# Four-layer fp32 block on one core: gates by tokens, output product by halves, convolutions by taps, head evacuations behind the norm

## The chip, the cores and the metric

The kernel runs on one core of a Trainium2 chip, as one launch. The metric is the device time of that launch in microseconds (us). Each core has a matrix engine, TensorE (PE), whose weight loads are listed apart (PEld), and VectorE (DVE), ScalarE (ACT), GpSimd (POOL) and SyncE (SP), which here issues all loads. PE writes its results to PSUM (the tiles called bank); everything else lies in SBUF.

## The reference, cut to what matters

The input is 256 tokens of width 1024 in fp32. It passes through two layers of one kind (here a0, a1) and two of another (b0, b1). Of each layer the part that the change touches is the mixer: a projection of the normed input feeds four branches, and the branches are merged by gates:

```python
# layers a: four branches of width 512
ys = jnp.stack([y_ssm, y_fox, y_moba, y_dsa], axis=2)
proj = jnp.einsum('bsnc,ncd->bsnd', ys, w_branch)
gates = jax.nn.sigmoid(h @ w_gate + b_gate).reshape(bsz, seq, N_BRANCH, D_MODEL)
merged = jnp.sum(gates * proj, axis=2)
return merged @ w_out

# layers b: four branches of width 256, gates without a bias
proj = jnp.einsum('bsnw,nwd->bsnd', branches, w_branch)
gate = jax.nn.sigmoid(gates).reshape(b, s, N_BRANCH, D_MODEL)
merged = jnp.sum(gate * proj, axis=2)
return merged @ w_out
```

In layers b one branch (deltanet) first runs a causal depthwise convolution of four taps and a silu over 768 channels, `silu(causal_depthwise_conv(concat(q, k, v), conv_w))`, and another (spatial gating) a gelu and `u * (mixed + b_s)`. After the mixer, layers a have a swiglu network, layers b a cross-attention over 256 memory tokens and a squared-relu network. Each sub-block begins with an rmsnorm.

## The kernel before, in words

**Products.** PE's fast fp32r form is not exact enough alone, so each fp32 product is made of three matmuls (`mm3`): low half of the left operand by high half of the right, high by low, high by high, all into one PSUM bank. Weights come from memory in chunks of two row tiles of 128 by 512 columns (512 KB) into one of a few `raw` buffers; ACT rounds a chunk to its high half (`high`, `rt<-raw`), DVE subtracts to get the low half (`low`, `rt<-raw,rt`), and PE uses the pair. Pairs are prepared `LOOK = 5` ahead, in the order of `plan`. Two loops use them. `g1` holds a tile of 128 tokens still and streams 512 weight columns: the result has tokens on partitions. `g2` holds 128 weight columns still and streams the 256 tokens: the result has channels on partitions.

**Order.** All instructions are emitted by one program that runs twice: a dry run gives the time at which each chunk is due, the second run emits. Between the matmuls of a product, `tick` prepares chunks (`advance`) and lets other work step forward: generators in named queues, "lanes" (`spawn`, `lane`), which yield where they would wait. `Model` holds a clock of each engine, and a lane steps when the model says that its inputs are there. A lane spawned with a key is stepped before `advance` does its part, and `flush(key)` runs it to its end. `scoped` runs something at once. `drain` runs lanes dry. Each engine executes its instructions in the order in which they were emitted.

**Stages of a layer.** `head` runs the first products of a mixer: for each of the two token halves it flushes the norm's lane of that half (`h0`, `h1`), runs `g1` on each named block and evacuates it at once. In layers a the blocks are misc (320 columns that get a rope, 16 and 4 more) and mq (512 columns, with a rope); `rope` is two multiplications on DVE from PSUM and an addition on POOL. Then come further blocks with the branches as lanes between them. `mix` runs over the four branches in a set order and two column halves c: `gate` (`g2`, 96 matmuls of 256 columns, then tanh on ACT, in layers a with a bias per channel, which is a bias per partition), `proj` (`g2` on the branch's output, DVE multiplies with the gate, POOL or DVE adds to the sum), and after the last branch `fin` splits the sum, which is in the form that the next product needs, into high and low halves. `out_a` and `out_b` run the output product by `g1` and `g11`, per column half c over all 8 row tiles, and flush `mT0` to `mT3` (the pieces of the sum) as they come to them.

**Convolutions and spatial gate in layers b.** `convs` runs `g2` for two groups of 128 channels and spawns `conv`: ACT writes the last tap, `acc = src * w3`, and DVE adds the three others, one operation per tap and group, each reading PSUM:

```python
for i in range(2):
    for j in (1, 2, 3):
        self.stt(av[:, i, j:], src[:, i, :256 - j], wts[i][:, 3 - j:4 - j], av[:, i, j:], OP.mult, OP.add)
self.fbank(bank)
```

There are three such convolutions a layer. `sgu` evacuates the spatial gate with four operations of 64 columns, one per group; `gelu` has two passes before its tanh.

**Lines and names.** All engine operations are recorded on line L362 (a helper), loads on L434. Tile names: `raw` a weight chunk, `rt` a high or low half, `ft` anything else in SBUF, `bank` PSUM, `qt` small matrices in another form, `junk` results that nobody reads. A row of 128x1024 with `rt<-raw,rt` on DVE is the low half of a whole chunk; 128x512 is half a chunk. The third layer of the kernel is b0.

## Time and profile before

| what | value |
|---|---|
| runs, median of 3 | 2286.72 us (2281.83 to 2288.86) |
| the profiled execution, its own time | 2281.47 us |
| its span on the core | 2279.7 us |
| mean granted PE clock | 0.993 |
| matmuls | 16244 |
| instructions | 40153 |
| read from memory | 371.81 MB |

The span is the time from the first to the last instruction that the hardware profiler recorded; the execution's own time has some 1.8 us around it. Busy times are given per engine, with the share of the span. A waiting engine is put down to the one whose semaphore came last. The granted clock is the share of full speed that PE was given: its two levels are 1.2 and 2.4 GHz, so a stretch at 0.65 holds both.

### The profile page before, as it was taken

The numbers are of one execution on the slowest core, as the hardware profiler recorded it, in microseconds if no ns is written. First come the engines' busy times: TensorE is split into PE (matmuls) and PEld (weight loads), VectorE is DVE, ScalarE is ACT, GpSimd is POOL, SyncE is SP. The second block draws the span as 40 slices with busy tenths as digits, with TensorE's granted clock in tenths as the row PEclk, the third lists the DMA queues.
The fourth block names the chain that finished last, engine by engine and source line by source line (L and its number), as shares of the span: only waits on it lengthen the run. The fifth ranks groups of instructions, "written<-read, shape, count | busy, mean of one in ns | idle before, by whom it ended". The sixth has DMA issues, their size and how long they took to land. (4 is left out here: it accounts for less than half of the span.)

```text
span 2279.7 us, 40153 instructions
## 1 busy us (share of the span) xinstructions
PE 2232.7 (98%) x16244; PEld 2015.1 (88%) x16244; DVE 1526.0 (67%) x2509; ACT 1073.2 (47%) x1695; POOL 267.0 (12%) x244
## 2 busy tenths in 40 slices
PE   8999999999899999999998999999999899999998
PEld 6888998999788899899888899988988889998897
DVE  7887567546798756665678767455567877745554
ACT  4555545434455554444454335454445433544543
POOL 2102110000301111000112220000001222000000
PEclk9999999999999999999999999999999999999999
DMA  6444565655444456565534256446653424644563
GB/s 228 149 130 148 163 196 183 206 193 164 147 130 139 148 172 203 197 211 179 167 112 149 77 162 207 157 151 234 205 157 106 153 80 157 207 162 151 194 206 109
DMA packets 106662, 375.47 MB, mean 165 GB/s; under 512 B 12474, under 2 KB 12908, under 8 KB 106476
## 3 DMA queue, kind: packets, MB, share of 16 engines
q1 hardware_dynamic: 106476, 372.91, 49.9%
q8 instruction: 127, 2.08, 0.4%
q14 instruction: 59, 0.48, 0.1%
HBM read 371.81 MB, written 1.05 MB: 164 GB/s over the span
## 5 line engine op out<-in xcount | busy, mean ns | idle before, releaser
L362 PE MATMUL bank<-rt 128*128 128x256 f32 (+2 forms) x12720 | 1996.2, 316 | 20.5 <-DVE rt L362 20.4
L362 PEld LDWEIGHTS bank<-rt 128*128 128x128 f32 x12720 | 1778.5, 192 | 176.1 <-DVE rt L362 26.7
L362 DVE TENSOR_TENSOR rt<-raw,rt 128x1024 fp32r<-128x1024 f32 (+2 forms) x692 | 834.0, 1229 | 347.2 <-ACT rt L362 345.8
L362 ACT ACTIVATE rt<-raw 128x1024 fp32r<-128x1024 f32 (+2 forms) x692 | 694.7, 1033 | 366.7 <-PE bank L362 211.8
L362 POOL TENSOR_TENSOR ft<-ft 128x512 f32<-128x512 f32 (+6 forms) x186 | 213.0, 1154 | 1847.4 <-DVE ft L362 1578.0
L362 PE MATMUL bank<-ft 64*64 64x64 f32 (+13 forms) x3476 | 312.9, 264 | 19.6 <-DVE ft L362 13.5
L362 PEld LDWEIGHTS bank<-ft 64*64 64x64 f32 (+6 forms) x3476 | 240.3, 146 | 78.1 <-DVE ft L362 19.6
L362 ACT ACTIVATE ft<-bank 128x512 f32<-128x512 f32 (+4 forms) x256 | 135.2, 536 | 305.2 <-PE bank L362 292.5
L362 ACT ACTIVATE ft<-ft 128x128 f32<-128x128 f32 (+7 forms) x206 | 87.5, 435 | 189.5 <-DVE ft L362 181.3
L362 DVE SCALAR_TENSOR_TENSOR ft<-ft 128x512 f32<-128x512 f32 (+5 forms) x211 | 93.1, 462 | 37.0 <-ACT junk L362 20.2
L362 DVE TENSOR_TENSOR ft<-ft 128x512 f32<-128x512 f32 (+5 forms) x122 | 69.9, 575 | 63.3 <-ACT ft L362 58.3
L362 ACT ACTIVATE rt<-bank 128x512 fp32r<-128x512 f32 (+1 forms) x98 | 53.5, 553 | 99.8 <-PE bank L362 99.4
L362 DVE SCALAR_TENSOR_TENSOR ft<-bank,ft 128x255 f32<-128x255 f32 (+6 forms) x176 | 80.2, 482 | 26.5 <-PE bank L362 10.0
L362 DVE TENSOR_TENSOR ft<-ft,bank 64x512 f32<-64x512 f32 (+3 forms) x92 | 59.4, 645 | 40.3 <-PE bank L362 37.0
L362 ACT ACTIVATE ft<-bank,ft 128x256 f32<-128x256 f32 x108 | 47.1, 480 | 78.8 <-PE bank L362 49.1
L362 DVE SCALAR_TENSOR_TENSOR ft<-ft,bank 128x512 f32<-128x512 f32 (+1 forms) x106 | 67.5, 641 | 19.7 <-PE bank L362 9.7
L362 ACT ACTIVATE rt<-ft 128x512 fp32r<-128x512 f32 x62 | 39.1, 630 | 81.1 <-DVE ft L362 76.6
L362 DVE COPY ft<-bank 128x384 f32<-128x384 f32 (+5 forms) x96 | 49.3, 541 | 31.4 <-PE bank L362 28.7
L362 DVE TENSOR_SCALAR ft<-ft 128x256 f32<-128x256 f32 (+7 forms) x236 | 56.7, 284 | 19.9 <-ACT ft L362 8.9
L362 DVE TENSOR_TENSOR ft<-bank,ft 128x512 f32<-128x512 f32 (+8 forms) x124 | 50.4, 442 | 18.4 <-PE bank L362 9.7
L362 DVE SCALAR_TENSOR_TENSOR rt<-bank,rt 128x512 fp32r<-128x512 f32 (+1 forms) x72 | 43.3, 612 | 17.2 <-ACT rt L362 17.0
L362 ACT ACTIVATE junk<-ft 128x512 bf16<-128x512 f32 (+1 forms) x46 | 27.2, 591 | 57.4 <-DVE ft L362 53.2
(37 smaller groups left out, 314.8 us busy)
## 6 DMA issues: line engine op xcount, KB each, us to landing
raw<-in_wts_a SPq DMA_DIRECT2D x340, 512.0 KB, 4.3
raw<-in_wts_b SPq DMA_DIRECT2D x312, 512.0 KB, 4.2
raw<-in_wts_b SPq DMA_DIRECT2D x24, 256.0 KB, 2.7
raw<-in_wts_b SPq DMA_DIRECT2D x8, 440.0 KB, 4.0
raw<-in_wts_a SPq DMA_DIRECT2D x8, 340.0 KB, 4.4
ft<-in_mem SPq DMA_DIRECT2D x4, 512.0 KB, 7.8
ft<-in_x SPq DMA_DIRECT2D x2, 512.0 KB, 3.4
ft<-in_norm_mix_pre SPq DMA_DIRECT2D x2, 512.0 KB, 5.3
```

The source lines that it names most:

```text
L362: r = None if self.dry else f(*args, **kw)
```

## The change

It has six parts.

1. **Gates and projections by tokens.** `mix` uses `g1` in place of `g2`: 48 matmuls of 512 columns in place of 96 of 256 for a gate. The bias now runs along columns, so it is loaded as a row to all partitions (`fetch`, 16 loads of 256 KB, one gate step before its use), added by DVE (`tt`) ahead of one tanh. The merged sum has tokens on partitions, so `fin` transposes it (`transpose_to`: four PE transposes per piece, 16 pieces, lanes `mT{c}{t}`).
2. **Output product by halves.** The chunks of w_out are cut by row halves r as well, and `out_a`, `out_b` run r outside c: the second column half of the sum is needed only for r = 1. `drain` before it leaves the keyed lanes alone.
3. **Convolutions by taps** in layers b: ACT scales each tap from PSUM (8 operations a convolution in place of 2), POOL makes three additions of 2 x (256 - j) columns, and DVE does only the last pass.
4. **Head evacuations as a lane.** In layers a each evacuation of a head block is spawned under the key "head" and yields once; the lane is flushed at the end of `head`. A clause in `rope` gives its addition to DVE while half 1 of the norm is under way.
5. **gelu**: one pass fewer on DVE (the factor goes into the Square).
6. **sgu**: one addition of 256 columns on DVE from PSUM and a multiplication on POOL in place of four operations of 64.

```diff
-        for c in range(2):
-            cb(f"o{c}", "w_out", (l,), full, [(c * 512, c * 512 + 512)])
+        for r in range(2):
+            for c in range(2):
+                cb(f"o{r}{c}", "w_out", (l,), (512 * r, 512 * r + 512), [(c * 512, c * 512 + 512)])
...
             self.g1(b[:, :width], layer, name, lhs, t, 4, t == 1)
-            self.scoped(evac, t, b)
+            if specs[0][0] == "misc":
+                self.spawn(self.later(evac, t, b), "head")
+            else:
+                self.scoped(evac, t, b)
+        self.flush("head")
+
+    def later(self, evac, t, b):
+        yield
+        evac(t, b)
...
-        self.tt(a.a[:, :n], a.a[:, :n], c.a[:, :n], OP.add, self.P)
+        self.tt(a.a[:, :n], a.a[:, :n], c.a[:, :n], OP.add, None if "h1" in self.keys.values() else self.P)
...
+    def conv_by_taps(self, bank, wts, dst):
+
+        F = self.F
+        src = view(bank, 2, 256)
+        acc, th, tap = (F.alloc(512, n) for n in ("cacc", "cth", "ctap"))
+        av = acc.v(2, 256)
+        for i in range(2):
+            self.act(av[:, i], src[:, i], AF.Copy, scale=wts[i][:, 3:4])
+        for j, u in ((1, th), (2, tap), (3, th)):
+            for i in range(2):
+                self.act(u.v(2, 256)[:, i, :256 - j], src[:, i, :256 - j], AF.Copy, scale=wts[i][:, 3 - j:4 - j])
+            if j == 3:
+                self.fbank(bank)
+            self.tt(av[:, :, j:], av[:, :, j:], u.v(2, 256)[:, :, :256 - j], OP.add, self.P)
+            yield
+        tap.free()
+        self.act(th.a, acc.a, AF.Tanh, scale=0.5)
+        yield
+        self.stt(dst, th.a, 1.0, acc.a, OP.add, OP.mult)
...
+        def fetch(s):
+            if bias is not None and s < len(steps):
+                n, c = steps[s]
+                rows[s] = self.row_at(bias, l, 512, "bg", n * D + c * 512)
+
+        def gate(s):
+            n, c = steps[s]
+            fetch(s + 1)
             out = []
-            for g in range(2):
+            for t in range(2):
                 b = self.bank()
-                self.g2([b[:, 0:256], b[:, 256:512]], L, f"g{n}{c}", hT, halves[g], 4, g == 1)
+                self.g1(b, L, f"g{n}{c}", hT, t, 4, t == 1)
                 gt = F.alloc(512, "gt")
                 if bias is None:
                     self.act(gt.a, b, AF.Tanh, scale=0.5)
                 else:
...
-                        self.act(gt.a[:, 256 * j:256 * j + 256], b[:, 256 * j:256 * j + 256], AF.Tanh, scale=0.5,
-                                 bias=bias[:, ch:ch + 1])
+                    self.tt(gt.a, b, rows[s].a, OP.add)
+                    self.act(gt.a, gt.a, AF.Tanh, scale=0.5)
...
-        def fin(c, g, s_):
-            yield from self.split(m[c], (slice(None), slice(2 * g, 2 * g + 2), slice(None)), s_.v(2, 256))
+        def fin(c, t, s_):
+            yield "pe"
+            yield from self.transpose_to(s_.a, 4, m[c], t)
             s_.free()
...
-                self.g2([b[:, 0:256], b[:, 256:512]], L, f"p{n}{c}", ys[n][0], halves[g], nkt // 2, g == 1)
-                gt = gts[g]
+                self.g1(b, L, f"p{n}{c}", ys[n][0], t, nkt // 2, t == 1)
+                gt = gts[t]
...
-            for c in range(2):
-                b = self.bank()
-                self.g1(b, L, f"o{c}", m, t, 4, t == 1, wait=lambda p: self.flush("mT%d" % p))
-                self.scoped(self.post_half, st, c, b, gp.a, 0.5)
+            bb = [self.bank(), self.bank()]
+            for r in range(2):
+                self.flush("mT%d%d" % (r, t))
+                for c in range(2):
+                    self.g1(bb[c], L, f"o{r}{c}", m, t, 2, t == 1, 4 * r, r == 0, r == 1)
+                    if r:
+                        self.scoped(self.post_half, st, c, bb[c], gp.a, 0.5)
...
-            self.act(x2.a, b, AF.Square)
-            yield
-            self.ts(x2.a, x2.a, 0.044715, OP.mult, 1.0, OP.add)
-            self.tt(x2.a, x2.a, b, OP.mult)
+            self.act(x2.a, b, AF.Square, scale=math.sqrt(0.044715))
+            yield
+            self.stt(x2.a, x2.a, 1.0, b, OP.add, OP.mult)
...
-                for g in range(4):
-                    sl = slice(g * 64, (g + 1) * 64)
-                    self.stt(sgv[:, t, sl], b[:, sl], sgb[:, g:g + 1], sgv[:, t, sl], OP.add, OP.mult)
+                s4 = F.alloc(256, "sgs")
+                self.tt(s4.v(4, 64), view(b[:, :256], 4, 64), sgb[:, :, None].to_broadcast([128, 4, 64]), OP.add)
                 self.fbank(b)
+                self.tt(sgv[:, t, 0:256], sgv[:, t, 0:256], s4.a, OP.mult, self.P)
...
-                self.spawn(self.conv(b, [cwt[:, c0 + 2 * g + j] for j in range(2)], None,
-                                     cv.v(3, 512)[:, c0 // 2 + g]), "conv")
+                self.spawn(self.conv_by_taps(b, [cwt[:, c0 + 2 * g + j] for j in range(2)],
+                                             cv.v(3, 512)[:, c0 // 2 + g]), "conv")
```

`out_b` is changed as `out_a` is, and a new array `b_gate` is passed. Because the order comes from the planner, the diff alone does not tell where instructions stand now. Three places follow, each as the order of the instructions on one engine (x4 means four alike in a row; the line of the helper is L362 before and L364 after).

PE, the last steps of the first layer's mix before (the gate and projection banks; a gate is two lots of 48, a projection two of 24):

```order
L362 MATMUL bank_72<-rt 128x256 x48
L362 MATMUL bank_69<-rt 128x256 x24
L362 MATMUL bank_74<-rt 128x256 x24
L362 MATMUL bank_73<-rt 128x256 x48
L362 MATMUL bank_75<-rt 128x256 x48
L362 MATMUL bank_68<-rt 128x256 x24
L362 MATMUL bank_71<-rt 128x256 x24
```

and with the change:

```order
L364 MATMUL bank_69<-rt 128x512 x24
L364 MATMUL bank_68<-rt 128x512 x24
L364 MATMUL bank_74<-rt 128x512 x12
L364 MATMUL bank_70<-rt 128x512 x12
L364 MATMUL bank_72<-rt 128x512 x12
L364 MATMUL bank_73<-ft 128x128 x4
L364 MATMUL bank_72<-rt 128x512 x9
L364 MATMUL bank_71<-ft 128x128 x4
```

Each lot has half as many matmuls of twice the columns, and between those of the last gate there stand lots of four transposes (128x128) of the first half of the sum.

DVE, the start of the second layer (320, 16 and 4 columns are the evacuation of misc, the two of 128x512 from a bank are mq's rope, the pair of `ISA` rows the norm's square sum, 128x1 and the last two of 128x512 its root and its last pass), before:

```order
L362 TENSOR_TENSOR rt<-raw,rt 128x1024 x3
L362 TENSOR_TENSOR ft<-bank_70,ft 128x320 x2
L362 TENSOR_TENSOR ft<-bank_70,ft 128x16
L362 TENSOR_SCALAR ft<-bank_70 128x4
L362 SCALAR_TENSOR_TENSOR ft<-ft 128x512 x2
L362 ISA junk,ft<-ft 128x512
L362 ISA ft 128x1
L362 TENSOR_TENSOR ft<-bank_71,ft 128x512 x2
L362 SCALAR_TENSOR_TENSOR ft<-ft 128x1
L362 SCALAR_TENSOR_TENSOR ft<-ft 128x512 x2
```

and with the change:

```order
L364 TENSOR_TENSOR rt<-raw,rt 128x1024 x3
L364 SCALAR_TENSOR_TENSOR ft<-ft 128x512 x2
L364 ISA junk,ft<-ft 128x512
L364 ISA ft 128x1
L364 SCALAR_TENSOR_TENSOR ft<-ft 128x1
L364 SCALAR_TENSOR_TENSOR ft<-ft 128x512 x2
L364 SCALAR_TENSOR_TENSOR rt<-bank_72,rt 128x4x128
L364 SCALAR_TENSOR_TENSOR rt<-bank_69,rt 128x4x128
L364 TENSOR_TENSOR ft<-bank_74,ft 128x320 x2
L364 TENSOR_TENSOR ft<-bank_74,ft 128x16
L364 TENSOR_SCALAR ft<-bank_74 128x4
L364 TENSOR_TENSOR ft<-bank_71,ft 128x512 x2
```

The evacuations of misc and mq stand behind the whole norm of half 1 and the low halves of its transposes. On POOL the rope's additions stay where they were, but the norm's root (128x1) now stands ahead of both.

DVE, the convolution stage of b0, before (64 columns are the spatial gate, 255 to 253 the taps):

```order
L362 TENSOR_TENSOR rt<-raw,rt 128x512
L362 SCALAR_TENSOR_TENSOR rt<-bank_71,rt 128x2x128
L362 SCALAR_TENSOR_TENSOR ft<-bank_69,ft 128x64 x4
L362 SCALAR_TENSOR_TENSOR ft<-bank_68,ft 128x255
L362 SCALAR_TENSOR_TENSOR ft<-bank_68,ft 128x254
L362 SCALAR_TENSOR_TENSOR ft<-bank_68,ft 128x253
L362 SCALAR_TENSOR_TENSOR ft<-bank_68,ft 128x255
L362 SCALAR_TENSOR_TENSOR ft<-bank_68,ft 128x254
L362 SCALAR_TENSOR_TENSOR ft<-bank_68,ft 128x253
L362 SCALAR_TENSOR_TENSOR ft<-ft 128x512
L362 TENSOR_TENSOR rt<-raw,rt 128x512
L362 TENSOR_TENSOR rt<-raw,rt 128x1024
```

and with the change:

```order
L364 TENSOR_TENSOR rt<-raw,rt 128x512
L364 SCALAR_TENSOR_TENSOR rt<-bank_73,rt 128x2x128
L364 TENSOR_TENSOR ft<-bank_71,ft 128x256
L364 COPY ft<-bank_74 128x384
L364 COPY ft<-bank_68 128x384
L364 TENSOR_TENSOR ft<-bank_72,ft 128x128
L364 TENSOR_TENSOR ft<-bank_73,ft 128x128
L364 SCALAR_TENSOR_TENSOR ft<-ft 128x512
L364 TENSOR_TENSOR rt<-raw,rt 128x512
L364 TENSOR_TENSOR ft<-ft 128x256
```

The taps are gone from DVE; between the spatial gate's one addition and the next weight half there now stand evacuations of another branch (384 and 128 columns), which came later before.

## Rows read from the trace of the kernel before

**Rows 1.** Page, part 1: busy time, share of the span and instructions by engine.

```profile
PE 2232.7 (98%) x16244; PEld 2015.1 (88%) x16244; DVE 1526.0 (67%) x2509; ACT 1073.2 (47%) x1695; POOL 267.0 (12%) x244
```

**Rows 2.** What PE waited for, whole run: total us, times, longest us.

```profile
PE bank L362 <- DVE rt L362: 20.4, 16, 4.2
PE bank L362 <- DVE ft L362: 13.5, 8, 7.4
```

**Rows 3.** PE by form, gates 282.95:294.35, product 352.0:362.7: xcount | busy, mean ns.

```profile
L362 PE MATMUL bank<-rt 128*128 128x256 f32 x97 | 11.8, 283 | 0.0
...
L362 PE MATMUL bank<-rt 128*128 128x512 f32 x48 | 11.1, 390 | 0.0
```

**Rows 4.** Timeline of PE: start us, us, engine, operation, xcount.

```profile
175.04 0.60 PE L362 MATMUL bank<-ft 128*128 128x128 f32 x4
175.40 0.94 PE L362 MATMUL bank<-rt 128*128 128x512 f32 x3
```

**Rows 5.** What PE waited for, convolution stage of each later layer.

```profile
PE bank L362 <- DVE rt L362: 6.7, 5, 4.2
...
PE bank L362 <- DVE rt L362: 6.1, 5, 4.2
```

**Rows 6.** Timeline of DVE in the third layer's convolution stage.

```profile
1202.49 3.69 DVE L362 SCALAR_TENSOR_TENSOR ft<-bank,ft 128x64 f32<-128x64 f32 x10
...
1206.71 1.82 DVE L362 TENSOR_TENSOR rt<-raw,rt 128x512 fp32r<-128x512 f32 x2
```

**Rows 7.** Timeline of PE in the same place: [idle before, releaser].

```profile
1207.44 6.43 PE L362 MATMUL bank<-rt 128*128 128x256 f32 x35 [4.17 <-DVE rt L362]
```

**Rows 8.** Windows: us, PE, PEld, DVE, ACT, POOL busy, granted clock, DMA share, GB/s.

```profile
1176.90:1213.00 36.10, 30.14 (x229) 29.43 (x228) 32.88 (x101) 16.20 (x36) 4.78 (x7) 0.91 0.34 110
1207.40:1213.90 6.50, 6.43 (x35) 6.23 (x35) 5.52 (x21) 3.48 (x8) 1.01 (x1) 0.65 0.52 161
```

**Rows 9.** DVE by form, window 1176.9:1213.

```profile
L362 DVE SCALAR_TENSOR_TENSOR ft<-bank,ft 128x254 f32<-128x254 f32 x6 | 2.9, 482 | 0.2
```

**Rows 10.** POOL, DVE by form, windows 1255:1302, 260:320 (POOL); 1560:1660, 260:320 (DVE).

```profile
L362 POOL TENSOR_TENSOR ft<-ft 128x512 f32<-128x512 f32 x8 | 10.3, 1286 | 20.9 <-PE bank L362 14.8 <-DVE ft L362 6.1
...
L362 POOL TENSOR_TENSOR ft<-ft 128x512 f32<-128x512 f32 x8 | 16.6, 2077 | 90.5 <-ACT rt L362 76.1 <-DVE ft L362 14.4
...
L362 DVE TENSOR_TENSOR rt<-raw,rt 128x1024 fp32r<-128x1024 f32 x35 | 41.8, 1223 | 20.8 <-ACT rt L362 20.7
...
L362 DVE TENSOR_TENSOR rt<-raw,rt 128x1024 fp32r<-128x1024 f32 x23 | 30.8, 1363 | 25.5 <-ACT rt L362 25.5
```

**Rows 11.** Timelines of DVE, POOL and PE at the second layer's head.

```profile
570.86 0.96 DVE L362 TENSOR_TENSOR ft<-bank,ft 128x320 f32<-128x320 f32 x3
...
575.75 1.29 DVE L362 TENSOR_TENSOR ft<-bank,ft 128x512 f32<-128x512 f32 x2 [1.18 <-PE bank L362]
...
578.99 1.41 DVE L362 SCALAR_TENSOR_TENSOR ft<-ft 128x512 f32<-128x512 f32 x2 [1.88 <-POOL ft L362]
...
577.19 1.77 POOL L362 TENSOR_TENSOR ft<-ft 128x512 f32<-128x512 f32 x2 [3.25 <-DVE ft L362]
...
579.80 1.75 PE L362 MATMUL bank<-ft 128*128 128x128 f32 x8 [4.08 <-DVE ft L362]
```

**Rows 12.** What PE waited for, same head, window 562:605.

```profile
PE bank L362 <- POOL ft L362: 2.1, 3, 1.2
```

**Rows 13.** Windows: first layer's mix, its end with the output product, third layer's branches.

```profile
201.70:259.80 58.10, 58.10 (x487) 54.41 (x486) 42.14 (x93) 31.83 (x71) 3.59 (x3) 1.00 0.54 164
317.40:374.70 57.30, 57.30 (x394) 53.40 (x393) 37.47 (x44) 28.13 (x41) 4.60 (x4) 1.00 0.59 188
1255.00:1302.00 47.00, 45.82 (x851) 42.08 (x850) 35.66 (x60) 13.76 (x23) 13.49 (x16) 1.00 0.31 92
```

**Rows 14.** Page, part 6: DMA issues, xcount, KB each, us to landing.

```profile
raw<-in_wts_b SPq DMA_DIRECT2D x24, 256.0 KB, 2.7
```

**Rows 15.** What SP's DMA queue waited for, whole run.

```profile
SPq L434 <- DVE ft L362: 182.2, 56, 22.0
```

92 lines of the change are left out of this document (50 added, 42 removed).

## The prediction, made before the changed kernel was run

> **What bounds the kernel now.** Read the busy shares first: TensorE (PE) is busy 98% of the span, the weight loads beside it 88%, VectorE (DVE) 67% [rows 1]. So the time is PE's own work plus the few places where PE stands still, and a change counts only if it shortens one or the other. The waits of PE say how much standing there is: 20.4 us for DVE's low halves of weights (tile rt) and 13.5 us for DVE's other results, 34 us for DVE together [rows 2]. Everything else is pace: what one matmul costs when the next follows at once. The profiled execution took 2281.47 us around a span of 2279.7 us; the median of the three runs is 2286.72 us, 5.2 us more. I sum differences against the profiled execution (its time would become 2251.8 us) and apply them to the median, since runs are what will be compared. A measurement of this kernel can tell about 0.3%, 6.9 us, from no change.
>
> **Gates and projections by tokens: -25.5 us of PE.** In a pure gate stretch 97 matmuls of 256 columns take 11.8 us, one alone being 0.283 us long: (11.8 - 0.283)/96 = 0.120 us each. In the output product 48 matmuls of 512 columns take 11.1 us: (11.1 - 0.390)/47 = 0.228 us each [rows 3]. Two of the first (0.240) do the work of one of the second, so the wider form saves 0.012 us a pair. A gate step goes from 96 x 0.120 = 11.52 to 48 x 0.228 = 10.94 us, -0.58; there are 8 steps in each of 4 layers: -18.6. A projection goes from 48 to 24 matmuls in the first two layers (5.76 to 5.47, 16 of them: -4.6) and from 24 to 12 in the last two (2.88 to 2.74, 16: -2.3). The trace shows both forms in long streaks, so this is the surest term.
>
> The Trainium skill speaks against it: TensorE: Matmul & The Clock Gate, section Back-to-back issue gap, gives columns/2.4 + 2.5 ns for a warm matmul, so 109 ns at 256 and 216 ns at 512. By that estimate a pair saves 2.5 ns, all 2112 pairs some 5.5 us, and the sum below would end near 2277 us. This trace disagrees at 256 columns (120 ns measured), so the rows decide.
>
> **The merge needs transposes now: +5.8 us.** The merged sum has tokens on partitions, so each of its 16 pieces (4 a layer) takes four PE transposes. The trace has such fours between 512-column matmuls: from their start at 175.04 to the next matmul at 175.40 is 0.36 us [rows 4]; 16 x 0.36 = 5.8. ScalarE (ACT) and DVE split the piece into halves as before, only from PSUM. PE's net work: -25.5 + 5.8 = -19.7.
>
> **Convolutions by taps: -9 us.** In both later layers PE stands still while the convolutions run: five waits for DVE's weights, 6.7 and 6.1 us together, the longest 4.2 us in each [rows 5]. The long one is easy to read. DVE begins at 1202.49 on ten small operations in a row (four of the spatial gate, six of a convolution), 3.69 us; only at 1206.71 does it reach the two weight halves [rows 6], and PE, idle for 4.17 us, starts at 1207.44 [rows 7]. PE pays twice: after the stall the granted clock is 0.65, a mix of its two levels, 1.2 and 2.4 GHz [rows 8], and 35 matmuls take 6.43 us [rows 7] instead of 35 x 0.12 = 4.2, 2.2 more.
>
> The change takes all 18 tap operations of a convolution off DVE in a layer (six of one width are 2.9 us [rows 9], so 18 are 8.7), makes one 256-wide addition of the spatial gate's four, and removes a 512-wide pass twice. ACT does 24 scalings a layer where it did 6. At the 0.48 us of DVE's like ones [rows 9] 18 more are 8.7 us, on an engine that is busy 16.2 of 36.1 us there [rows 8]: hidden, but the chains behind get longer. POOL takes nine 512-wide additions a layer. Such an addition takes 1.29 us in the branches of the later layers and 2.08 us in the merge, beside DVE's weight halves; a weight half, 1.22 us where POOL does nothing, takes 1.36 there [rows 10]. So the two slow each other, and nine additions give DVE's freed time partly back: 9 x 0.14 = 1.3 us at least, 9 x 1.29 = 11.6 us at most, more than was freed. Bounds: nothing, to all of the stalls and the slow clock behind them, 6.7 + 6.1 + 2 x 2.2 = 17.2, say -17. I take the middle: the 4.2 and the 2.2 behind it shrink to 2.0 (-4.4 a layer, -9 in all; nearest to rows 6, where the ten operations leave the queue; by the new order evacuations of another branch move up into their place, so not all of it goes), and the short waits stay.
>
> The Trainium skill, SBUF - State Buffer, section SBUF: two separate sides, says why: DVE with two SBUF inputs and GpSimd share a port pair under an exclusive lock, the loser blocking for the whole instruction. The mutual slowing above agrees in direction. By the full lock this term would be nothing and the sum 2266 us.
>
> **The head block behind the norm's steps: -4 us.** At the start of the second layer PE waits 4.08 us for token half 1 of the norm. DVE first evacuates the misc block (0.96 us), then works on the residual, then rotates mq (1.29), and the norm's last pass starts at 578.99 after 1.88 us of waiting for POOL, which does mq's addition and only then the norm's root, 1.77 us together [rows 11]. The change lets these evacuations yield, so they stand behind the norm's steps. What comes off the chain is 0.96 + 1.29 and most of 1.88, some 4 us. Between nothing and that wait with the POOL waits of the stretch (4.1 + 2.1 = 6.2 [rows 12]). What is late next: the transposes of misc and mq, which wait for POOL 2.1 us already and move later with their evacuation. The clause that would give rope's additions to DVE while half 1 is under way catches none: they stand on POOL's queue as before, only behind the root. Nothing.
>
> **What it adds elsewhere: +3 us.** The same rule holds in the first layer, whose norm waits for the input itself, so that nothing is won; pushing work back can only make something late there: between nothing and +4, the other layer's gain with its sign turned; I take +2. The 32 bias additions on DVE cost 0.65 us each (two like reads of a bank with a tile are 1.29 [rows 11]), 20.6 in all, but in the merge of the first layers DVE is busy 42.1 of 58.1 us at its fullest, and three gate steps add 6 x 0.65 = 3.9 to that [rows 13]: hidden; without that cover up to 20.6. ACT does one pass of 512 in place of two of 256. The 16 rows of the bias are loads of 256 KB, which land in 2.7 us [rows 14], issued a gate step (11 us and its projection) ahead: hidden. The output product by halves has as many matmuls, and PE is busy 57.3 of 57.3 us from the last gate steps through it today [rows 13]: no stall to win; the added transposes lengthen the last merge, covered by the first half's 24 matmuls (24 x 0.228 = 5.5 us): nothing to 4 x 0.6, I take +1. Draining only the unkeyed lanes before the product issues nothing new: nothing. The gelu's two passes in one are in the freed DVE time above.
>
> **Sum.** -19.7 - 9 - 4 + 3 = -29.7; 2286.7 - 29.7 = **2257 us**. Ends: -19.7 - 17 - 6.2 = -43 (2244); -19.7 + 4 + 2.4 = -13 (2273); and half the spread of the runs, 3.5 us, at either end: 2240 to 2277.
>
> **The rivals.**
> - *POOL's additions lock DVE out.* What leaves DVE comes back as blocked time, and the convolution stage keeps its stalls: 2257 + 9 = 2266 us. For: rows 10. Against: the same additions run at 1.29 us where DVE is busy 35.7 of 47.0 us [rows 13]. 22%.
> - *The evacuations wait their turn too long.* The wait for the norm goes, those for misc, mq and the weights behind them take its place, in both first layers: 2257 + 4 + 4 = 2265 us. For: the head's POOL waits [rows 12]. Against: they are half the norm's. 12%.
> - *The wide form pays no better.* If a 512-column matmul ran at 0.240 us in the gates, TensorE's work would not shrink and the transposes would stay: 2257 + 25.5 = 2282 us. Against: rows 3. 4%. The page's issue gap, above, is a milder form of it.
> - *Slower: the bias rows block the load queue.* SP issues every load in order and waits for the buffer to be free; it waited for DVE to free ft buffers 56 times, up to 22.0 us [rows 15]. A bias row goes into a freshly freed buffer, and all weight loads stand behind it. It decides once a block outlasts the five chunks prepared ahead, 5 x 2.9 = 14 us of gate work (a chunk is a quarter of a step); if then each of the 16 rows shows its landing, 16 x 2.7 = 43: 2257 + 43 = 2300 us. Against: the two gain rows loaded in the same place today leave PE no idle time [rows 13]. 5%.
>
> **The numbers.** The forecast keeps 57%. Its own range with the first two rivals holds over 8 in 10: 2240 to 2277. Faster by over 0.3%: 57 + 22 + 12%, 0.91; within: the third and a little more, 0.05; slower: 0.04.
>
> **What would show it.** Right: gate steps of 10.9 us, 48 matmuls of 512 columns each; no PE wait near 4 us for weights before the first gate of the later layers, and granted clock 1.00 there; the wait at the second layer's head under 1 us; 64 more transposes at 0.09 us. POOL's additions of 510 elements at 1.3 us would favour the forecast, above 2 us the first rival. Wrong: 512-column matmuls in the gates above 0.235 us, or PE waits on DVE's weights in the convolution stage as long as before.

## The result and the profile after

The changed kernel takes **2270.81 us** (median of 4 runs, 2268.53 to 2272.47) against 2286.18 us (4 runs, 2281.83 to 2288.86) for the kernel before: a ratio of 0.9935 with a 95% interval from 0.9921 to 0.9949, so 15.4 us or 0.65% faster. The forecast was 2257 us, 29.7 us faster; the range from 2240 to 2277 us holds the time. The sign was right, half of the gain did not come. That the range holds it is in part luck: its slow end was made of other losses (convolutions and heads that gain nothing, dearer transposes) than those that came. The profiled execution took 2268.53 us around a span of 2266.7 us, 13.0 us less span than before; the differences below are made between these two executions.

The busy times and the waits of PE of the changed kernel, which answer to [rows 1] and [rows 2]:

```profile
PE 2220.7 (98%) x14196; PEld 1897.8 (84%) x14196; DVE 1532.2 (68%) x2487; ACT 1077.9 (48%) x1699; POOL 293.1 (13%) x266
```

```profile
PE bank L364 <- DVE rt L364: 21.6, 16, 3.8
PE bank L364 <- DVE ft L364: 9.6, 6, 7.2
```

PE is busy 12 us less, and DVE's weights, 20.4 us of waiting before, are waited for no less: 21.6 us. The forecast took 19.7 us of work off PE, and some slow clock, which counts as busy, besides; and it took waits for DVE's weights away. Part of the work went, of these waits nothing. They stand in other places now.

To find where, cut PE's timeline at the first matmul of each stage, in both kernels. The table gives the time of each stage before, the difference in the changed kernel, and what the forecast's terms make of it:

| stage (both layers together) | before | changed | forecast |
|---|---|---|---|
| first layers: head, blocks and branches | 385.3 | +0.1 | -2 |
| first layers: gates, projections, output product | 346.6 | -10.7 | -10.5 |
| first layers: swiglu | 385.8 | +3.8 | 0 |
| later layers: convolution stage | 72.5 | -8.8 | -9 |
| later layers: gates, projections | 346.3 | +0.8 | -8.2 with the next |
| later layers: output product | 47.2 | +2.1 | |
| later layers: all else | 679.2 | -0.3 | 0 |
| sum | | -13.0 | -29.7 |

(-10.5 is 2 x (4.64 + 2.30) for the form, less 3.4 for half of the transposes and of the 1 us behind them; -8.2 is 2 x (4.64 + 1.15) less the same 3.4.) The first layers' mixers and the convolution stage are as forecast to 0.2 us. The later layers' mixers and products are 11.1 us short of it, the swiglu 3.8, the heads 2.1.

Two cautions belong to the table. It compares one execution of each kernel, and that of the kernel before was as fast as the fastest of its runs; a stage whose PE and POOL instructions have the same order in two kernels differed by up to 1.7 us (the first head, before and with "the yields on the kernel before", below). And a stage begins at the first matmul of a weight product, while the matmuls of the branches move: in the changed kernel 84 of them stand in each convolution stage where 36 stood, and 48 fewer in the mixer behind. So stage and mixer are best taken together: 8.0 us less in both later layers, with the output product 5.9, against a forecast of 17.2.

Windows of the gates and projections of the first layer and of the third, in the changed kernel and in the one before (columns as in [rows 8]):

```profile
204.40:348.60 144.20, 144.20 (x688) 116.25 (x687) 105.01 (x158) 73.58 (x116) 20.36 (x11) 1.00 0.61 200
...
1202.00:1375.70 173.70, 169.05 (x1500) 131.50 (x1499) 124.74 (x207) 71.85 (x114) 52.54 (x43) 0.97 0.45 146
```

```profile
201.70:352.00 150.30, 150.30 (x1256) 146.61 (x1255) 95.92 (x144) 75.66 (x130) 20.21 (x11) 1.00 0.58 181
...
1213.00:1387.00 174.00, 172.01 (x2022) 161.13 (x2021) 124.75 (x196) 67.87 (x104) 47.68 (x43) 0.99 0.46 143
```

In the first layer PE is busy all the time at full clock in both kernels, 144.2 in place of 150.3 us. In the third PE has 522 matmuls less, but the stage is as long as before, and the granted clock is 0.97 where it was 0.99 (the fourth layer: 173.4 and 172.5 us, 0.97 and 1.00). The matmuls' own price is as forecast: in a pure stretch of gates

```profile
L364 PE MATMUL bank<-rt 128*128 128x512 f32 x103 | 23.5, 389 | 0.0
```

(23.5 - 0.389)/102 = 0.227 us each, against the 0.228 of the sum. So something stands in the later mixers that was not there. PE's timeline of the changed kernel there, and then the granted clock in two windows, of the stretch behind the wait and of the convolution stage:

```profile
1202.57 4.30 PE L364 MATMUL bank<-rt 128*128 128x512 f32 x17 [0.18 <-DVE rt L364]
...
1208.01 0.49 PE L364 MATMUL bank<-rt 128*128 128x512 f32 x1
1211.27 0.73 PE L364 MATMUL bank<-rt 128*128 128x512 f32 x2 [2.77 <-DVE rt L364]
...
1216.23 1.63 PE L364 MATMUL bank<-rt 128*128 128x512 f32 x3
```

```profile
1211.30:1222.30 11.00, 10.88 (x53) 8.09 (x54) 5.63 (x15) 3.94 (x8) 3.21 (x4) 0.55 0.30 97
1170.20:1202.00 31.80, 31.13 (x278) 29.54 (x276) 24.06 (x64) 18.83 (x48) 15.64 (x17) 1.00 0.34 108
```

The convolution stage (the last row: PE busy 31.13 of 31.80 us, clock 1.00) is clean now. PE's idle time in it fell from 6.0 us [rows 8] to 0.7, and the clock rose from 0.91 to 1.00, worth (1 - 0.91) x 36.1 = 3.2 us. Of these 8.5 us a layer the stage gained 4.3; the other 4.2, by this estimate, went to the 48 matmuls that moved in. But the first gate starts at 1202.57, after 18 of its matmuls PE waits 2.77 us for a weight half, and then runs for 11 us at a granted clock of 0.55: three matmuls of 512 columns take 1.63 us from the first's start to the last's end, where three take 0.93 in the second layer's head. The wait costs 2.8 us, the slow clock behind it (1 - 0.55) x 11 = 5.0; how much of this is the wait's doing, the yields show below. Before, the wait of 4.17 us [rows 7] and 6.5 us at 0.65 [rows 8] stood in the convolution stage, ahead of the first gate. What DVE does meanwhile is the reading that matters most, its timeline in the changed kernel:

```profile
1204.17 1.22 DVE L364 TENSOR_TENSOR rt<-raw,rt 128x1024 fp32r<-128x1024 f32 x1
...
1205.64 0.71 DVE L364 TENSOR_TENSOR ft<-ft 128x8 f32<-128x8 f32 x1
...
1207.93 1.37 DVE L364 SCALAR_TENSOR_TENSOR ft<-ft 128x8 f32<-128x8 f32 x7
...
1209.42 0.64 DVE L364 SCALAR_TENSOR_TENSOR ft<-ft 128x8 f32<-128x8 f32 x3
1209.99 1.23 DVE L364 TENSOR_TENSOR rt<-raw,rt 128x1024 fp32r<-128x1024 f32 x1
```

Between the weight half at 1204.17 and the one at 1209.99 DVE works off 18 operations of 8 columns, nearly all of them the softplus of the deltanet branch, from 1205.64 to 1209.99: 4.3 us for almost no data. The half that PE waits for is the next one in DVE's queue. The row of small operations was there before too, from 1208.44 on, but PE was then still slow and late from the convolutions, and waited 0.62 us behind it.

In the second layer's head the timelines of DVE and PE show what was forecast (before: [rows 11]):

```profile
571.87 1.41 DVE L364 SCALAR_TENSOR_TENSOR ft<-ft 128x512 f32<-128x512 f32 x2 [0.73 <-POOL ft L364]
...
575.27 0.96 DVE L364 TENSOR_TENSOR ft<-bank,ft 128x320 f32<-128x320 f32 x3
...
574.74 3.05 PE L364 MATMUL bank<-rt 128*128 128x340 f32 x18 [0.75 <-DVE rt L364]
...
599.11 0.66 PE L364 MATMUL bank<-ft 128*128 128x128 f32 x4 [1.73 <-POOL ft L364]
```

The norm's last pass comes after 0.73 us of waiting, misc's evacuation stands behind it, and PE's wait of 4.08 us is 0.75. What is late next are transposes that wait 1.73 us for POOL.

The swiglu of the second layer has a wait that was not forecast. Timelines of PE, DVE and SP's load queue:

```profile
973.78 11.40 PE L364 MATMUL bank<-rt 128*128 128x256 f32 x80 [3.78 <-DVE rt L364]
...
955.88 0.17 DVE L364 CAST ft<-ft 128x2 f32<-128x2 int32 x1 [5.94 <-DMA ft<-in_positions]
...
961.77 3.49 DVE L364 TENSOR_TENSOR rt<-raw,rt 128x1024 fp32r<-128x1024 f32 x3
...
948.32 0.42 SPq L436 DMA_DIRECT2D ft<-in_positions  x1
961.32 0.33 SPq L436 DMA_DIRECT2D ft<-in_norm_mix  x1
...
965.75 19.56 SPq L436 DMA_DIRECT2D raw<-in_wts_a  x10
```

Here the third layer's parameters are loaded. DVE has the positions in front of it: it stands idle for 5.94 us until they have landed, does the rope's table, and reaches the next weight half at 961.77. SP stops at 948.7 for a buffer that DVE frees only at 961.3, and issues weights again at 965.75. PE waits 3.78 us. Before, DVE's idle time there was 6.07 us, and PE's longest wait 1.8. One thing that differs is how long SP is held up: the next weight load is issued 17.4 us after the positions (965.75 less 948.32), before it was 14.9:

```profile
958.70 0.42 SPq L434 DMA_DIRECT2D ft<-in_positions  x1
...
973.62 18.48 SPq L434 DMA_DIRECT2D raw<-in_wts_a  x10
```

Before, four of the eight small loads were out ahead of the stop, now none is.

### The profile page after: what moved, and what is told of

Read it like the earlier page. It is cut to its first block, busy times and chain, and to the rows that moved or that the text cites. A ratio compares the mean times of both kernels' runs of the same rounds, so it can differ in the third digit from the quotient of the medians.

```text
span 2266.7 us, 36067 instructions
## 1 busy us (share of the span) xinstructions
PE 2220.7 (98%) x14196; PEld 1897.8 (84%) x14196; DVE 1532.2 (68%) x2487; ACT 1077.9 (48%) x1699; POOL 293.1 (13%) x266
## 4 chain that ended last, share of the span: by engine, by line
PE 87%; DVE 6%; issue 2%; POOL 2%; ACT 1%; DMA 1%; SPq 0%; POOLq 0%; DVEq 0%; ACTq 0%
PE bank L364 87%; DVE ft L364 4%; DVE rt L364 2%; POOL ft L364 2%; DMA raw<-in_wts_a 1%; ACT ft L364 1%; ACT rt L364 1%; DMA ft<-in_positions 0%; DMA ft<-in_norm_mix 0%; ACT junk L364 0%; DVE junk L364 0%; SPq L436 0%; POOLq L2733 0%; POOLq L364 0%; DVEq L364 0%
## 5 line engine op out<-in xcount | busy, mean ns | idle before, releaser
L364 PE MATMUL bank<-rt 128*128 128x512 f32 (+3 forms) x10608 | 1977.8, 344 | 21.8 <-DVE rt L364 21.6
L364 PEld LDWEIGHTS bank<-rt 128*128 128x128 f32 x10608 | 1649.1, 190 | 255.9 <-DVE rt L364 28.5
L364 DVE TENSOR_TENSOR rt<-raw,rt 128x1024 fp32r<-128x1024 f32 (+2 forms) x692 | 833.6, 1229 | 293.2 <-ACT rt L364 291.9
L364 ACT ACTIVATE rt<-raw 128x1024 fp32r<-128x1024 f32 (+2 forms) x692 | 695.8, 1034 | 343.5 <-PE bank L364 159.5
L364 POOL TENSOR_TENSOR ft<-ft 128x512 f32<-128x512 f32 (+10 forms) x208 | 241.6, 1173 | 1835.3 <-DVE ft L364 1271.9
L364 PE MATMUL bank<-ft 64*64 64x64 f32 (+13 forms) x3540 | 328.2, 266 | 17.3 <-DVE ft L364 9.6
L364 PEld LDWEIGHTS bank<-ft 64*64 64x64 f32 (+7 forms) x3540 | 252.4, 147 | 102.4 <-issue 35.0
L364 ACT ACTIVATE ft<-bank 128x512 f32<-128x512 f32 (+4 forms) x256 | 135.0, 537 | 310.7 <-PE bank L364 273.7
L364 ACT ACTIVATE ft<-ft 128x128 f32<-128x128 f32 (+7 forms) x238 | 107.5, 462 | 252.9 <-DVE ft L364 235.7
L364 DVE TENSOR_TENSOR ft<-ft 128x512 f32<-128x512 f32 (+5 forms) x122 | 72.2, 596 | 64.9 <-ACT ft L364 62.4
L364 DVE SCALAR_TENSOR_TENSOR ft<-ft 128x512 f32<-128x512 f32 (+5 forms) x211 | 92.7, 460 | 30.9 <-ACT junk L364 15.7
L364 ACT ACTIVATE rt<-bank 128x512 fp32r<-128x512 f32 (+1 forms) x114 | 63.1, 558 | 103.5 <-PE bank L364 97.9
L364 DVE TENSOR_TENSOR ft<-bank,ft 128x512 f32<-128x512 f32 (+8 forms) x160 | 74.1, 490 | 46.3 <-PE bank L364 34.8
L364 DVE SCALAR_TENSOR_TENSOR ft<-ft,bank 128x512 f32<-128x512 f32 (+1 forms) x110 | 70.4, 643 | 33.7 <-PE bank L364 18.5
L364 DVE TENSOR_TENSOR ft<-ft,bank 64x512 f32<-64x512 f32 (+3 forms) x88 | 56.6, 643 | 41.6 <-PE bank L364 38.6
L364 DVE TENSOR_SCALAR ft<-ft 128x256 f32<-128x256 f32 (+7 forms) x230 | 60.2, 305 | 25.6 <-ACT ft L364 9.8
L364 DVE SCALAR_TENSOR_TENSOR ft<-bank,ft 128x256 f32<-128x256 f32 (+5 forms) x124 | 60.4, 508 | 24.2 <-PE bank L364 10.8
L364 DVE COPY ft<-bank 128x384 f32<-128x384 f32 (+5 forms) x96 | 49.3, 541 | 30.4 <-PE bank L364 26.2
L364 ACT ACTIVATE junk<-ft 128x512 bf16<-128x512 f32 (+1 forms) x46 | 27.2, 591 | 68.0 <-DVE ft L364 65.2
L364 POOL TENSOR_SCALAR qt<-qt,ft 64x256 fp32r<-64x256 f32 (+1 forms) x32 | 36.0, 1129 | 125.5 <-PE bank L364 124.6
L364 DVE TENSOR_TENSOR rt<-bank,rt 128x512 fp32r<-128x512 f32 x42 | 28.9, 688 | 34.2 <-ACT rt L364 34.1
L364 DVE SCALAR_TENSOR_TENSOR rt<-bank,rt 128x512 fp32r<-128x512 f32 (+1 forms) x72 | 43.1, 610 | 13.0 <-ACT rt L364 12.8
```

Of the source, the lines that this page charges most:

```text
L364: r = None if self.dry else f(*args, **kw)
```

## The experiments

All ratios are to the kernel before, with 95% intervals; stage times are differences to the kernel before, as in the table above. The kernel before was run again beside each set of runs and took 2285.4 to 2287.1 us. The first four take the change apart, with the hunks shown ahead of the prediction.

**Taps alone** (parts 3, 5 and 6 on the kernel before):

```diff
-                self.spawn(self.conv(b, [cwt[:, c0 + 2 * g + j] for j in range(2)], None,
+                self.spawn(self.conv_by_taps(b, [cwt[:, c0 + 2 * g + j] for j in range(2)],
```

> The kernel before with the convolutions by taps, the gelu and the spatial gate of the change, and nothing else. Theory 'the wait moves': the stall of the convolution stage goes (-4.3 us a layer up to the first gate, as the changed kernel shows), but PE then reaches the first gates before DVE has their weight halves, waits there and has the low clock there, so that the mixers lose about the same: 2284 to 2288 us, and a wait for DVE's weights of over 2 us in the first gate of both later layers. Rival 'the taps are worth what was forecast, and the gates by tokens spoil it': 2277 us, no such wait.

2282.77 us, ratio 0.9989 (0.9979 to 1.0000): hardly faster. The convolution stage gains 7.5 us, a little less than with the whole change; the mixers behind, with 48 matmuls fewer each, lose 2.4. The rest loses 3.2 in places that the part does not touch, 1.8 of it in the heads, where PE's order is that of before. Of the later layers' mixers one gains 1.8 and one loses 4.2; in the latter PE's longest waits are 1.7 us for DVE's weights and 2.1 for its other results. No wait for weights is over 2 us there, so the theory is half right here: the time is near its number, the shape of the loss is not.

**Gates alone** (parts 1 and 2):

```diff
-                self.g2([b[:, 0:256], b[:, 256:512]], L, f"g{n}{c}", hT, halves[g], 4, g == 1)
+                self.g1(b, L, f"g{n}{c}", hT, t, 4, t == 1)
```

> The kernel before with the gates and projections by tokens and the output product by halves, without taps and without the head lane. Theory 'the wait moves': the first two layers' mixers gain 6 to 7 us each and lose 1.0 in the product, as in the changed kernel; the later mixers gain their 5 us too, since PE is held up in the convolution stage as before and DVE is not behind in the gates: -20 us, 2266 us, better than the changed kernel. Rival 'the form is what the later layers don't stand': their mixers take 173 us as before, -10 us, 2276 us.

2274.55 us, 0.9957 (0.9941 to 0.9973). The first layers gain 9.7 us and the later mixers 8.1, so the form is not at fault. Its waits in the third layer, from the convolution stage to the end of the mixer, are those of before [rows 5]:

```profile
PE bank L364 <- DVE rt L364: 6.5, 4, 4.2
```

The 20 us of the theory do not come: the later mixers with their products gain 6.0 us where it had 10, the first layers' heads lose 2.1 us and the swiglus 2.5.

**Head lane alone** (part 4):

```diff
+            if specs[0][0] == "misc":
+                self.spawn(self.later(evac, t, b), "head")
```

> The kernel before with the lane of the head blocks alone. Theory 'it comes back within the stage': the second layer's head gains 6 us at mq and loses 4 of them by the end of the stage, the first layer's loses 2.7: 2286 us, within 2 us of the kernel before. Rival 'the late weights in the second layer's swiglu (+3.5 us) come from it': 2290 us, with a second wait of 3.8 us there. The forecast's own terms (-4 and +2) would give 2284 us.

2296.52 us, 1.0054 (1.0039 to 1.0069): slower by 11 us, which neither theory had. The heads of the first two layers gain 1.3 us as a whole, the swiglus lose 2.6. The loss is 14.4 us in the mixers of the later layers, whose code is that of before. The order of their instructions is not: the planner places every lane by its model's clocks, which the new order in the first layers has shifted. Windows of the two later mixers (174.0 and 172.5 us before), and PE's waits in the first:

```profile
1213.40:1393.00 179.60, 173.48 (x2020) 162.06 (x2019) 124.58 (x196) 67.35 (x104) 46.27 (x43) 0.98 0.44 138
1793.00:1974.00 181.00, 176.31 (x2020) 164.79 (x2020) 124.83 (x197) 67.20 (x105) 45.25 (x43) 0.96 0.42 138
```

```profile
PE bank L362 <- POOL ft L362: 4.4, 2, 2.7
```

A wait for POOL of 2.7 us has come up in either (1.2 and 1.1 before), and the clock is lower than before. What is measured of one part alone can thus carry over 10 us that come from other layers' order.

**The change without the head lane** (parts 1, 2, 3, 5, 6):

```diff
-            if specs[0][0] == "misc":
-                self.spawn(self.later(evac, t, b), "head")
-            else:
-                self.scoped(evac, t, b)
+            self.scoped(evac, t, b)
```

> The changed kernel without the lane of the head blocks (and without rope's clause). Theory 'the lane is worth nothing over its stages': 2269 to 2273 us, like the changed kernel. If the swiglu's wait came with the lane it goes here: 2267 us. If the lane is worth the forecast's -2: 2273 us.

2272.55 us, 0.9947 (0.9932 to 0.9962): 1.7 us more than the changed kernel, with intervals that overlap. Its later layers show the interaction: the gates alone gain 8.1 us in the mixers; gates and taps together lose 1.4 there, while the convolution stage gains 8.7, 7.3 us in all. So next to the gates the taps bring nothing in these stages; alone they brought 5.1. In both later layers PE has a wait of 2.8 us for weights, as in the changed kernel, and PE, DVE and POOL have the changed kernel's order there, so the head lane has no part in it. The heads take 3.0 us more than with the lane. The swiglu's +3.3 is here too, so the lane is not needed for it.

**Cutting the row of small operations** (the changed kernel; a lane may now yield in the 8-column softplus too):

```diff
-        if n > 64:
+        if n != 32:
             yield
...
-            if n > 64 and k in (13, 7):
+            if n != 32 and k in (13, 7):
                 yield
```

> The changed kernel, with deltanet's softplus (17 operations of 8 columns in a row on DVE, 4.3 us, between two weight halves) cut in three by yields, as the larger softplus of the other branch is already. Theory 'this row of small operations is what makes the first gate's weights late': the wait of 2.8 us there and the low clock behind it (some 5 us) go in both later layers, 2271 - 14 = 2257 us, their mixers at 166 us in place of 173.7. Rival 'the taps' scalings and additions make the halves late, or the weights are simply behind by then': the wait stays within 1 us of 2.8 or turns up one chunk later, 2268 to 2272 us.

2260.41 us, 0.9883 (0.9866 to 0.9899): 10.4 us less than the changed kernel, by two lines that change only the order. The same stretch of DVE and PE:

```profile
1208.87 1.22 DVE L364 TENSOR_TENSOR rt<-raw,rt 128x1024 fp32r<-128x1024 f32 x1
...
1212.72 1.22 DVE L364 TENSOR_TENSOR rt<-raw,rt 128x1024 fp32r<-128x1024 f32 x1
...
1210.14 1.45 PE L364 MATMUL bank<-rt 128*128 128x512 f32 x5 [0.31 <-DVE rt L364]
...
1211.92 5.76 PE L364 MATMUL bank<-rt 128*128 128x512 f32 x24
```

The weight half stands in the middle of the row (1208.87), PE waits 0.31 us in place of 2.77, and 24 matmuls of 512 columns take 5.76 us, 0.24 each. The later mixers gain 8.0 us, and the convolution stage keeps its 8.7. With the products this is the forecast's time for these stages but for 2.8 us (-8.7 - 8.0 + 2.3 = -14.4 against -17.2). Against the changed kernel, with the same matmuls in them, the mixers are 3.6 and 5.3 us shorter: that is what the wait of 2.8 us and the clock behind it cost there. The swiglus, whose order is the changed kernel's, take 6.2 us more than before.

**Seven chunks ahead** in place of five (the changed kernel):

```diff
-LOOK = 5
+LOOK = 7
```

> The changed kernel with seven chunks prepared ahead in place of five. Theory 'a stock of halves outlasts the row of small operations': three quarters of the wait in the first gates goes, 2260 us. Rival 'ACT and DVE can't get further ahead in the convolution stage, since they are busy': the wait stays, 2271 us; halves made earlier may also stand ahead of the lanes' own operations and make those late, up to 2280 us.

2266.38 us, 0.9911 (0.9896 to 0.9925): between the two, but not by the later layers. PE's longest wait for weights in the third layer's mixer is 1.8 us in place of 2.8, yet stage and mixer together are 3.4 us longer than in the changed kernel over both layers, and the first layers' mixers 2.4. The gain stands in the heads (4.0 us) and the swiglus (5.7). It may be that halves made earlier stand ahead of the lanes' operations, which was not followed up. It does not tell the theories apart.

**The taps' additions on DVE** (the changed kernel):

```diff
-            self.tt(av[:, :, j:], av[:, :, j:], u.v(2, 256)[:, :, :256 - j], OP.add, self.P)
+            self.tt(av[:, :, j:], av[:, :, j:], u.v(2, 256)[:, :, :256 - j], OP.add)
```

> The changed kernel with the nine additions of the taps a layer on DVE in place of POOL. Theory 'the additions on POOL cost DVE little, DVE's queue is what matters': nine times about 0.65 us more on DVE bring the stalls of the convolution stage back in part, 2274 to 2280 us. Rival 'POOL's additions block DVE for their whole length': DVE is no later than before, the small operations beside them shrink, 2264 to 2271 us.

2264.90 us, 0.9904 (0.9890 to 0.9919): 5.9 us faster than on POOL, which is the rival's side. And the rival's mechanism is in the trace. DVE's operations by form in the convolution stage, of the changed kernel:

```profile
L364 DVE TENSOR_TENSOR rt<-raw,rt 128x512 fp32r<-128x512 f32 x8 | 5.5, 683 | 1.7 <-ACT rt L364 1.7
...
L364 POOL TENSOR_TENSOR ft<-ft 128x510 f32<-128x510 f32 x3 | 3.9, 1291 | 3.3 <-ACT ft L364 3.3
L364 DVE TENSOR_SCALAR ft<-ft 128x256 f32<-128x256 f32 x8 | 3.6, 456 | 0.1
...
L364 DVE SCALAR_TENSOR_TENSOR ft<-ft 128x512 f32<-128x512 f32 x1 | 1.2, 1162 | 0.0
```

and with the additions on DVE:

```profile
L364 DVE TENSOR_TENSOR rt<-raw,rt 128x512 fp32r<-128x512 f32 x8 | 5.2, 681 | 0.0
...
L364 DVE TENSOR_SCALAR ft<-ft 128x256 f32<-128x256 f32 x6 | 2.1, 350 | 0.1
...
L364 DVE SCALAR_TENSOR_TENSOR ft<-ft 128x512 f32<-128x512 f32 x1 | 0.7, 685 | 0.0
```

With POOL's additions in the stage (1.29 us each) DVE's operations on SBUF tiles take 0.456 and 1.162 us on the mean, without them 0.350 and 0.685; the weight halves take 0.683 and 0.681. That does not make the halves immune: of the eight only one starts while an addition runs, 0.16 us before its end. In the second layer's head of the changed kernel they do meet (timelines of DVE and POOL):

```profile
578.49 1.21 DVE L364 TENSOR_TENSOR rt<-raw,rt 128x1024 fp32r<-128x1024 f32 x1
...
579.63 2.31 DVE L364 TENSOR_TENSOR rt<-raw,rt 128x1024 fp32r<-128x1024 f32 x1
...
578.71 2.14 POOL L364 TENSOR_TENSOR ft<-ft 128x512 f32<-128x512 f32 x1 [1.16 <-PE bank L364]
```

The first half is under way when the addition starts: it takes its 1.21 us, and the addition 2.14. The second starts while the addition runs and ends 1.08 us behind it (581.93 against 580.85). So it is in the whole trace: 37 whole halves start with a POOL operation of 128 columns or more on two tiles still running for over 0.15 us, and each ends 1.08 us behind its end, after 1.23 to 2.32 us; 31 during which such an operation starts take 1.22, like those that meet none. Whichever starts second waits for the first.

The convolution stage is 4.3 us shorter than in the changed kernel, but 58 matmuls of the branches a layer have moved from it into the mixers, which are as long; stage and mixers together are 4.6 us shorter. Whether DVE is the better engine is asked again in the last experiment, without the row.

**Parameters ahead of the positions** (the changed kernel):

```diff
-                load_consts(layers[i + 1][0])
                 nxt_h["p"] = k.params(layers[i + 1])
+                load_consts(layers[i + 1][0])
```

> The changed kernel with the loads of the third layer's parameters ahead of its constants and of the positions. In the changed kernel eight small loads wait in the load queue from 948.7 to 961.3 us for DVE to free a buffer, which itself waits for the positions to land, and the swiglu's weights stand behind them (four loads waited so before the change). Theory 'the queue makes those weights late': the wait of 3.8 us there goes with the low clock behind it, second swiglu at 195 us in place of 198.5, 2266 us. Rival 'DVE's own work on the positions is what is late': 2271 us.

2279.13 us, 0.9969 (0.9956 to 0.9982), 8 us slower than the changed kernel. SP no longer waits 12 us for a buffer ahead of the parameters, but the positions are issued later, DVE stands behind them, and the weights come later still:

```profile
957.58 0.33 SPq L436 DMA_DIRECT2D ft<-in_positions  x1
970.37 18.49 SPq L436 DMA_DIRECT2D raw<-in_wts_a  x10
```

So this order of the loads does not cure it. It does not clear the load queue either, for the positions now stand 9 us later in it; DVE's wait for the positions is the better candidate, and the last experiment but one takes that away. Most of the loss is in the fourth layer, whose convolution stage and mixer take 6.8 us more than in the changed kernel: there the row of small operations has come to stand ahead of two halves in the convolution stage, and PE waits 5.1 us.

**The yields on the kernel before**:

```diff
-        if n > 64:
+        if n != 32:
             yield
...
-            if n > 64 and k in (13, 7):
+            if n != 32 and k in (13, 7):
                 yield
```

> The kernel before with deltanet's softplus cut in three by yields, and nothing else. Theory 'the row of small operations only bites where PE comes early': before, PE is held by the convolutions until 1207.4 us and waits for weights behind the row for 0.6 and 0.2 us, so that the yields are worth 1 to 2 us, 2285 us. Rival 'the row costs the same in either kernel': -10 us as in the changed one, 2277 us.

2284.46 us, 0.9996 (0.9986 to 1.0006): no difference that can be measured. The row costs nothing as long as PE is held up by the convolutions.

**The yields with the old convolutions** (the changed kernel with parts 3, 5 and 6 undone, and the yields):

```diff
-                self.spawn(self.conv_by_taps(b, [cwt[:, c0 + 2 * g + j] for j in range(2)],
+                self.spawn(self.conv(b, [cwt[:, c0 + 2 * g + j] for j in range(2)], None,
```

> The changed kernel with the yields and the old convolutions, gelu and spatial gate. Theory 'the taps' forecast was right but for the wait behind them': with the row cut they are worth their 9 us, and undoing them gives 2260 + 9 = 2269 us, with the wait of 4.2 us before the first gates again. Rival 'the taps are worth nothing, the yields do it all': 2260 us.

2271.17 us, 0.9932 (0.9916 to 0.9949), 10.8 us slower than with the taps. PE waits 4.2 us for weights in both convolution stages again, as the theory has it. With the row cut the taps are worth what was forecast and a little more; with the row whole they gave 2.0 us (gates alone against gates with taps, both without the head lane). The yields gave 1.1 us on the kernel before, 10.4 on the changed one.

**The yields and the rope's table in a lane** (the changed kernel; weight halves may pass the wait for the positions):

```diff
+        def tables():
+            t0 = self.model.clk["PE"]
+            while self.model.clk["PE"] < t0 + 9000.0:
+                yield
...
+        self.spawn(tables(), "tab")
```

> The changed kernel with the yields, and with the table of the third layer's rope (26 small operations on DVE that begin by waiting 5.9 us for the positions to land) made by a lane that starts 9 us after the load and yields three times; weight halves may go ahead. Theory 'DVE stands in order behind the positions, and the second swiglu's weights behind DVE': the waits of 3.5 and 1.1 us there go and the low clock behind them, second swiglu at 190 to 193 us in place of 199, 2254 us. Rival 'the loads are late in their own queue': 2260 us.

**2250.57 us**, 0.9843 (0.9826 to 0.9861): the fastest kernel here, 20 us less than the changed one. DVE and PE in the second layer's swiglu, and the windows of the two later mixers:

```profile
953.14 3.50 DVE L364 TENSOR_TENSOR rt<-raw,rt 128x1024 fp32r<-128x1024 f32 x3 [0.52 <-ACT rt L364]
957.38 0.17 DVE L364 CAST ft<-ft 128x2 f32<-128x2 int32 x1 [0.74 <-DMA ft<-in_positions]
...
963.51 1.22 DVE L364 TENSOR_TENSOR rt<-raw,rt 128x1024 fp32r<-128x1024 f32 x1
...
951.50 33.72 PE L364 MATMUL bank<-rt 128*128 128x256 f32 x236
```

```profile
1196.10:1363.40 167.30, 164.75 (x1501) 128.25 (x1500) 123.96 (x207) 71.76 (x114) 49.58 (x43) 1.00 0.46 152
1759.60:1926.80 167.20, 164.67 (x1501) 128.19 (x1500) 123.88 (x207) 71.84 (x114) 49.53 (x43) 1.00 0.48 152
```

Three weight halves stand ahead of the positions' first operation, which waits 0.74 us for the load in place of 5.94, and 236 matmuls follow one another without a wait. The second swiglu takes 3.7 us less than before where it took 3.5 more. The mean granted clock of the run is 0.998 (0.993 in the changed kernel), 1.00 in both later mixers, which take 167.3 and 167.2 us: 11.9 us less than before. Convolution stage, mixers and products together are 18.2 us shorter, against the forecast's 17.2. Of the 11.2 us that the profiled execution gains on that of the yields alone, 8.0 are in the swiglus and 3.8 in the mixers; why the mixers gained was not followed up.

**The same with the taps' additions on DVE**:

```diff
-            self.tt(av[:, :, j:], av[:, :, j:], u.v(2, 256)[:, :, :256 - j], OP.add, self.P)
+            self.tt(av[:, :, j:], av[:, :, j:], u.v(2, 256)[:, :, :256 - j], OP.add)
```

> As the one before, with the taps' additions on DVE. Theory 'POOL's additions make DVE's operations on SBUF tiles wait beside them, so that they are dearer on POOL': 4 us less than the one before, as in the changed kernel, 2250 us. Rival 'what the additions on DVE gained was only where the row of small operations fell': the same as the one before within 2 us, or up to 4 us more.

2260.98 us, 0.9888 (0.9870 to 0.9906): 10 us slower than on POOL. Again 58 matmuls a layer move behind the end of the convolution stage: it is 4.4 us shorter, the mixers 14.1 longer, both together 9.8 longer, where with the row whole they became 4.6 shorter. So POOL is the right engine once the row is cut, although DVE's operations wait for its additions where they start second. The rival is nearer than the theory, and outside its number; what in the mixers is late was not followed up (PE's waits there are 1.0 us at most).

## Why the prediction was right and where it was wrong

The price of the new form and the mechanism of the head lane were right. The sum missed half of the gain because one step failed, that the short waits of the later layers would stay as they were, and because a stage that it does not name became longer.

**The form of the gates and projections: right.** 0.227 us per matmul against 0.228, and 10.7 us in the first layers against 10.5 with the transposes. The Trainium skill, TensorE: Matmul & The Clock Gate, section Back-to-back issue gap, gives the formula that the prediction quotes for an isolated matmul; by it this would have been 5.3 us in all four layers together (2112 x 2.5 ns; the prediction has 5.5). The trace disagrees with that, and the rows that were taken in its place were the right ones.

**The transposes and the product by halves: right where it can be read.** There are 64 matmuls of 128x128 more, 728 against 664. In the first layers the products take 2.0 us more and the mixers gain 1.1 less than the form's 13.9, 3.1 of the 3.4 us that were taken for these layers. In the later layers the products take 2.1 us more; in their mixers the waits cover the rest.

**The head lane: right in its mechanism, smaller in size.** The wait of 4.08 us became 0.75. Early in the second layer's head PE is 6.4 us ahead of the kernel before, at the first gate 2.5: the rest is lost again on the way, part of it to transposes that wait for POOL, which the text had named as late next. The first layer lost 2.6 us where 2 were taken; but the change without the lane loses 3.3 there and the kernel before with the yields 1.7, so this loss is not shown to be the lane's. Against the change without it, the lane gains 0.7 and 2.4 us in the two heads. By the medians the lane is worth 1.7 us, with intervals that overlap, where -4 + 2 was said; alone it cost 11, through the later layers' order.

**The convolutions by taps: the step that failed.** The term was -9 us, and the stage gained 8.8, but this agreement is luck: the stage lost nearly all of its waits and its slow clock, some 17 us in both layers and so the upper bound of the term, and half of that was filled by matmuls that moved in from the mixers, which did not become shorter by it. The step that failed is the sentence that "the short waits stay". They did not: the waits behind the convolutions were short because PE was late. Once PE came 4.3 us earlier a layer, the operations that stood next in DVE's queue ahead of a weight half became the bound: 2.8 us of waiting with slow clock behind it, 3.6 and 5.3 us in the two layers by the run without it. The text asked of every stall what is late next in the second layer's head, and not here, where DVE's timeline of before has the 8-column operations right behind the weight halves (from 1208.44 on). Shown by the runs: with the row cut the taps are worth 10.8 us, with the row whole 2.0.

**The gates in the later layers** were forecast at -8.2 us with the product, and came to +2.9: the same wait. Alone they gave -6.0, and in the whole change with the row cut -5.7, there with 48 matmuls fewer in each mixer.

**Not forecast: the second layer's swiglu, +3.5 us.** A place that no part of the change touches, costed at nothing without being named. The waits of before there, up to 1.8 us, showed that it stood on the edge. Shown by the last experiment but one: with weight halves ahead of DVE's wait for the positions it is gone. Why it is longer with the change is open; it came with the head lane alone (+2.6 in both swiglus) and with the gates alone (+2.5). SP's stop goes with it: from the positions to the next weight load it takes 14.9 us before, 17.2 with the gates alone, 17.4 in the changed kernel and 9.1 with the table in a lane.

**The rivals.** "POOL's additions lock DVE out" gives 2266 us and was nearest to the time, for a reason that is not the one measured: seven of the nine additions in the third layer took 1.1 to 1.3 us, as in the forecast (the others 1.5 and 2.0), the convolution stage lost its stalls, and moving them to DVE is slower once the row is cut. The Trainium skill, SBUF — State Buffer, section SBUF: two separate sides, has it that a DVE operation with two SBUF inputs and a POOL operation that reads SBUF exclude each other, and that the one that starts first keeps the other out for its whole length. The trace agrees: the half that started second ended 1.08 us behind the addition, after 2.31 us, and the one that started first took 1.21. What kept the rival from coming true is that of the stage's eight halves only one started while an addition ran. "The evacuations wait too long" did not come true in size. The bias rows blocked nothing: both first mixers have PE busy all the time.
